# Two heads' final retention states multiplied out in the last norm, and y's last piece stored as two

## The chip, the cores and the metric

The kernel runs on one core of one Trainium2 chip. The metric is device time in microseconds (us) of one execution. The kernel before takes 1508.17 us (median of 3 runs, 1507.63 to 1508.33). One further execution was profiled; it took 1509.1 us. In the profile, PE is the matmul engine (TensorE), PEld its weight loads, DVE is VectorE, ACT ScalarE, POOL GpSimd and SP the engine that issues every DMA of this kernel. Nearly every instruction carries the line L318, the line of a recording helper, so instructions are told apart by tile names and shapes.

## The reference

One layer of a hybrid decoder over 16 meta tokens, 256 prompt tokens and 8 x 4 sample tokens. A norm and one input projection feed two groups of heads, RWKV-7 time mixing (16 heads, handled in 8 pairs) and retention (4 heads of width 256). Their outputs go through one output projection and a residual add, then a norm, a SwiGLU feed-forward with residual, and a last norm whose result is y. The states of all heads are outputs too. The part that matters here is the final retention state of the prompt:

```python
def retention_chunk(q, k, v, S, log_gamma):
    ...
    o_inter = jnp.einsum('bihd,bhde->bihe', q, S) * inter_scale[None, :, :, None]
    k_scale = jnp.exp(log_gamma[:, None] * (C - 1.0 - idx)[None, :])
    S_new = jnp.exp(log_gamma * C)[None, :, None, None] * S + jnp.einsum('bjhd,hj,bjhe->bhde', k, k_scale, v)
    return o_intra + o_inter, S_new

y_prompt = rms_norm(h_p, norm_final)[:, N_META:]
```

Since the prompt starts from a zero state, the last state of a head is one sum over all 272 prompt positions of decayed k times v: a 256 x 256 matrix per head. No other value of the step is computed from it.

## The kernel before, in words

Activations stand feature-major: 128 features on the partitions, tokens along the free axis (304 with the meta tokens, 288 without). All large products are made of 128 x 128 weight tiles. The weights come as one stream `big` in pieces of 128 x 512 (`wr`), five buffers deep; ACT rounds a piece to a short float (`wh`), DVE takes the rest (`wl`), and three matmuls per tile (`wh` with high and low part of x, `wl` with the high part) add up in a PSUM tile `acc`. `mm` are the other PSUM tiles (six banks), and nearly all other SBUF tiles lie in one arena (`arena_dt.float`, and `arena_dt.float32r` for rounded ones).

The order of work is written by a planner in a dry run (`Plan`). One main program walks through the weight stream: input projection, output projection in two halves (over the first 8 and the last 8 feature tiles of the mixed outputs), then for each of 11 groups the gate, up and down products. All other work, for example `pair(p)` for two RWKV heads and `ret(h)` for one retention head, is a stream, a generator with a rank. Whenever PE would take its next step, the planner lets the ready stream of lowest rank go on, and the main program only when none is ready. `RRANK` holds the ranks of the four retention heads; pair p has rank 1 + p. What results is one fixed order per engine. Arena places are chosen afterwards from the lifetimes.

`ret(h)` runs as follows. It transposes k and v on PE; ACT writes them to SBUF as `kt` (k scaled by the decay) and `vt`. PE makes the scores (six matmuls, 256, 144 and 48 columns wide, twice each); DVE multiplies q by the decay (`qh`), and ACT spreads it into `qz`. Then six matmuls of 128 x 256 in full fp32 give kt times vt in one `mm` bank, the final prompt state: ACT copies it to `so` and SP stores it in `rtp` (256 KB a head). `s0r` are the 8 samples' given states (four loads of 512 KB a head): sixteen matmuls of 32 x 256 multiply `qz` with them, the first four of each eight with the first half of `qz`. After that come the head's own outputs (two tiles `o`), a norm and the gate. The heads 2 and 3 run at the end of the input projection, together with the last pairs; the first product of the output projection begins when pair 7 is done, and its eight tiles of x are rounded (`xh`, `xl`) just ahead of it.

The end: the feature tile 15 of the last down product is added to the residual in three parts, each is squared on ACT, and `rstd_from` sums the squares over the features with matmuls one column wide, six in number, takes a square root (ACT) and a reciprocal (DVE), and spreads the result over all partitions with three matmuls of 96 columns. `bridge(n)` issues n products of ones with ones of 128 columns, whose result nothing reads: four of them stand ahead of the six, one behind them. Then `final` multiplies y's 16 feature tiles by the result on DVE, in 9 pieces (two of one tile, seven of two), and SP stores each piece when it is done.

Of the kernel before, what the change touches and what calls it, by code (L numbers as in the profile page):

```python
# [15 lines left out]
P = 128  # L16
D = 2048
KT = D // P
# [13 lines left out]
RD = 256  # L32
# [9 lines left out]
ACC = 2  # L42
LATE = 20000
WARM = 10
BRIDGE = 4
WR = 5
WCOLS = 512
WS = 5
# [1 line left out]
PMAX = 4  # L50
AHEAD = 4
RETS = 2
HELD = 2
RAHEAD = 2
RSTART = (-1, -1, 6, 5)
RRANK = (20, 21, 22, 2.5)
ORDER = "p0 p1 p2 r0 g0 p3 p4 r1 p5 p6 p7 g1 r2 g2 g3 r3"


# [548 lines left out]
class Step:  # L608


    def __init__(self, tc, I, O, ctx, rooms, draft, log):
        self.tc, self.nc, self.I, self.O = tc, tc.nc, I, O
        self.rooms, self.draft = rooms, draft
        pool = lambda n, b, **k: ctx.enter_context(tc.tile_pool(name=n, bufs=b, **k))
        self.lp = pool("lows", 1)
        self.cp = pool("const", 1)
        self.wp = pool("weights", 1)
        self.mp = pool("scratch", 1)
        self.ap_ = pool("acc", ACC, space=bass.MemoryType.PSUM)
        self.pp = pool("psum", 1, space=bass.MemoryType.PSUM)  # L620
        self.n, self.tags = 0, {}
        self.plan = pl = Plan(self.nc, rooms, draft, log, (lambda i: i) if draft else tc.keep_in_program_order)
        self.sp = pl.sp
        if not draft:
            self.arena = {dt: self.mp.tile([P, -(-(r.size - 16) // 64) * 64 + 16 if dt == F32 else r.size], dt, tag=f"arena_{dt}", name=f"arena_{dt}")
                          for dt, r in rooms.items()}
        self.pe, self.dve, self.act, self.pool = pl.pe, pl.dve, pl.act, pl.pool
        pl.outside = {v.name for v in (*I.values(), *O.values())}
        self.outs, self.later, self.held = [], [], []
        self.live = 0  # L630
        self.done = set()
        self.filled = set()
# [910 lines left out]
    def new_state(self, h, b2, s0, skh, svh):  # L1543
# [16 lines left out]
            dve.scalar_tensor_tensor(sd, sd, self.gam4[h], pt, op0=ALU.mult, op1=ALU.add)  # L1560
        self.put(self.O["rts"][h, b2], s0)

    def held_states(self, h, ks, vt):

        skh, svh = yield from self.exact(ks, vt)
        for b2 in range(NB // 2):
            s0 = self.t([P, 2, 2, RD], "s0n")
            self.sp.dma_start(s0, self.I["s0r"][h, b2])
            yield
            yield from self.new_state(h, b2, s0, skh, svh)  # L1570

    def ret(self, h, q, k, v):
        cst, act, dve, pe = self.cv, self.act, self.dve, self.pe
# [15 lines left out]
        kt = self.t([P, 3, RD], "kt")  # L1589
        vt = self.t([P, 3, RD], "vt")  # L1590
        ks = self.t([P, RD], "ks")
        sam = slice(P - 32, P)
        for src in k, v:
            for tiles in (0, 1), (2,):
                pt = self.ps(2 * len(tiles) + 1 if src is v else 3 * len(tiles) + (2 in tiles))
                for j, i in enumerate(tiles):
                    for d in range(2):
                        c = j * RD + d * P
                        pe.transpose(pt[:, c:c + P], src[:, d, KEYS[i][0]:KEYS[i][0] + P], ident)
                yield  # L1600
                if src is v:
                    n = len(tiles)
# [13 lines left out]
        pt = self.ps(7)  # L1616
# [8 lines left out]
        for d in range(2):  # L1625
            act.copy(qz[:, d, :, :4], four(qh[:, d]))

        pt = self.ps(7)
        for d in range(2):
            for i in range(3):  # L1630
                pe.matmul(pt[:, d * RD:(d + 1) * RD], kt[:, i, d * P:(d + 1) * P], vt[:, i, :],
                          start=i == 0, stop=i == 2)
        yield
        so = self.t([P, 2, RD], "so")
        act.copy(so, pt.rearrange("p (d e) -> p d e", d=2))
        self.put(self.O["rtp"][h], so)

        now = h < HELD
        if now:
# [2 lines left out]
        for g in range(2):  # L1642

            pt = self.ps(9)
            for d in range(2):
                for j in range(4):
                    b = 4 * g + j
                    pe.matmul(pt[32 * j:32 * j + 32, :RD], qz[:, d].rearrange("p b c -> p (b c)")[:, 32 * b:32 * b + 32], s0s[b // 2][:, d, b % 2, :],
                              start=d == 0, stop=d == 1, tile_position=(0, 32 * j))
# [16 lines left out]
        for e in range(2):  # L1666
            es = slice(e * P, (e + 1) * P)
            pt = self.ps(5)
# [63 lines left out]
            yield  # L1732
            self.dve.tensor_add(ssq, ssq, sq)

    def rstd_from(self, ssq, uses, more=None):


        ps = self.ps(4 if more is None else 7)
        n = TO // 3
        for c in range(3):  # L1740
            self.pe.matmul(ps[:n, c:c + 1], ssq[:, c * n:(c + 1) * n], self.ones[:, :1], start=True, stop=more is None)
            if more is not None:
                self.pe.matmul(ps[:n, c:c + 1], more[:, c * n:(c + 1) * n], self.ones[:, :1], start=False, stop=True)
        if more is None:
            yield
            rs = yield from self.rsqrt(ps[:n, :3], 1.0 / D, RMS_EPS)
        else:
            self.bridge(1)
            yield
            rs = self.t([n, 3], "rsz")  # L1750
            self.act.activation(rs, ps[:n, :3], AF.Sqrt, scale=1.0 / D, bias=self.eps[RMS_EPS][:n])
            yield
            self.dve.reciprocal(rs, rs)
            yield
        ps = self.ps(3 + uses)
        for c in range(3):
            self.pe.matmul(ps[:, c * n:(c + 1) * n], rs[:, c:c + 1].to_broadcast([n, P]), self.cv("id", n, 0, n),
                           start=True, stop=True)
        yield
        return ps[:, :TO]  # L1760

    def bridge(self, n=BRIDGE):

        pt = self.ps(n)
        for _ in range(n):
            self.pe.matmul(pt[:, :P], self.ones, self.ones, start=True, stop=True)

    def fill(self, k):

# [63 lines left out]
    def ffn_jobs(self):  # L1833
# [25 lines left out]
        def down_post(m, fin):  # L1859
            def g(acc):  # L1860
                hm = self.ht[m // 4][:, m % 4, :]
                if fin and m == KT - 1:

                    sq = self.t([P, TO], "sq2")
                    third = [slice(c * TO // 3, (c + 1) * TO // 3) for c in range(3)]
                    for c in third:
                        dve.tensor_add(hm[:, c], hm[:, c], acc[:, c])
                    for c in third:
                        act.activation(sq[:, c], hm[:, c], AF.Square)
                    self.bridge()  # L1870
                    yield
                    yield from self.final(sq)
                    return
                dve.tensor_add(hm, hm, acc[:, :TO])
                if fin:
                    if m == 0:
                        self.ssq3 = self.t([P, TO], "ssq3")

                        root = self.t([P, 1], "root")
                        act.activation(root, self.ones[:, :1], AF.Sqrt)  # L1880
                    yield
                    yield from self.sumsq(self.ssq3, hm, m == 0)
                    yield
                    act.activation(hm, hm, AF.Copy, scale=self.pv("gfin", m))
            return g
# [11 lines left out]
                                need=lambda f=f1 - 1 - (f1 == FT): ("act", f) in self.done))  # L1897
        return jobs

    def final(self, sq):  # L1900
        rstd = yield from self.rstd_from(self.ssq3, 9, sq)
        hm = self.ht[-1][:, 3, :]
        self.act.activation(hm, hm, AF.Copy, scale=self.pv("gfin", KT - 1))
        for m, n in [(0, 1), (1, 1)] + [(m, 2) for m in range(2, KT, 2)]:
            h = self.ht[m // 4][:, m % 4:m % 4 + n, :]
            self.dve.tensor_mul(h, h, rstd[:, None, :].to_broadcast([P, n, TO]))
            self.sp.dma_start(self.O["y"][:, m:m + n, :], h)

    def build(self, gam4):
        self.gam4 = gam4  # L1910
# [78 lines left out]
```

## Time and profile before

| what | value |
|---|---|
| three timed runs | 1508.17, 1507.63, 1508.33 us |
| profiled execution | 1509.1 us, of which the span from first to last instruction 1507.3 us |
| granted TensorE clock, mean | 0.997 |
| PE busy | 1493.5 us, 99% of the span, 11438 matmul records |
| DVE, ACT, POOL busy | 1086.2, 884.7, 31.9 us |
| chain of work that ended last | PE 95%, DVE 3%, ACT 1% |
| DMA | 258.57 MB, mean 172 GB/s |

A full fp32 matmul leaves two records in the profile, so a row with x12 is six matmuls. Rows of the timeline merge neighbouring instructions of one kind and name the first one's shape: a row "128x256" may hold matmuls of 144, 48 or 32 columns that follow it. A row's start is exact; the end of a matmul is modelled, so what a group of matmuls takes is read from its start to the start of the next row. In the text, pitch means this.

### The profile page before, as it was taken

The page shows a single profiled execution, that of the slowest core. Times are in us where ns is not written, and L with a number is a line of the kernel's source. Part 1 is how long each engine was busy: PE and PEld are TensorE (multiplying, and loading weights), DVE is VectorE, ACT ScalarE, POOL GpSimd, SP SyncE. Part 2 cuts the span into 40 slices and gives each one's busy share as a digit, 9 for nine tenths or more (in the row PEclk, how much of TensorE's full clock was granted, in tenths as well). Part 3 has the DMA queues.
Part 4 walks back from the last instruction along what each step waited for, and adds up shares of the span by engine and source line. Part 5 has one row for each costly group of instructions (what it writes and reads, how often), then busy time and mean ns, then how long its engine had stood idle before and what let it go on. Part 6 is the DMA issues. An engine that isn't in the chain of part 4 may idle for free.

```text
span 1507.3 us, 31980 instructions
## 1 busy us (share of the span) xinstructions
PE 1493.5 (99%) x11438; PEld 1475.3 (98%) x11438; DVE 1086.2 (72%) x2768; ACT 884.7 (59%) x2109; POOL 31.9 (2%) x165
## 2 busy tenths in 40 slices
PE   9999999999999999999999999999999999999997
PEld 8999999999999989999999999999999999999997
DVE  6989997999999668876656555656565656565657
ACT  6786778787875875567544444444444444444445
POOL 0010000000000000000000000000000000000000
PEclk9999999999999999999999999999999999999998
DMA  7545444545444368866655555555555555555563
GB/s 233 180 144 162 148 155 118 163 156 152 141 123 141 103 226 288 282 179 203 194 173 170 168 175 171 169 177 164 174 168 171 172 170 170 177 165 177 165 176 119
DMA packets 138784, 258.57 MB, mean 172 GB/s; under 512 B 16257, under 2 KB 22657, under 8 KB 138625
## 3 DMA queue, kind: packets, MB, share of 16 engines
q1 hardware_dynamic: 138624, 256.52, 55.8%
q8 instruction: 91, 1.49, 0.4%
q14 instruction: 69, 0.56, 0.1%
HBM read 242.18 MB, written 14.28 MB: 170 GB/s over the span
## 4 chain that ended last, share of the span: by engine, by line
PE 95%; DVE 3%; ACT 1%; issue 0%; DMA 0%; SPq 0%; DVEq 0%; ACTq 0%
PE acc L318 84%; PE mm L318 11%; DVE arena_dt.float L318 2%; ACT arena_dt.float L318 1%; DVE wl L318 1%; DMA arena_dt.float<-xT 0%; SPq L318 0%; ACT wh L318 0%; ACT arena_dt.float32r L318 0%; DVE arena_dt.float32r L318 0%; DVE xl L318 0%; DVEq L1985 0%; ACT xh L318 0%; ACT shout L318 0%; DVEq L318 0%
## 5 line engine op out<-in xcount | busy, mean ns | idle before, releaser
L318 PE MATMUL acc<-xh,wh 128*128 128x288 f32 (+2 forms) x2592 | 781.1, 301 | 1.5 <-ACT wh L318 1.5
L318 PE MATMUL acc<-xh,wl 128*128 128x288 f32 (+2 forms) x2592 | 763.9, 295 | 0.5 <-DVE wl L318 0.5
L318 PE MATMUL acc<-xl,wh 128*128 128x288 f32 (+2 forms) x2592 | 760.5, 293 | 0.0
L318 ACT CAST wh<-wr 128x512 fp32r<-128x512 f32 (+1 forms) x827 | 504.0, 617 | 347.9 <-PE acc L318 305.0
L318 DVE TENSOR_TENSOR wl<-wr,wh 128x512 fp32r<-128x512 f32 (+1 forms) x827 | 559.9, 686 | 125.7 <-ACT wh L318 121.0
L318 PEld LDWEIGHTS acc<-xh,wh 128*128 128x128 f32 x2592 | 486.7, 188 | 5.7 <-issue 2.7
L318 PEld LDWEIGHTS acc<-xl,wh 128*128 128x128 f32 x2592 | 486.3, 188 | 3.0 <-issue 1.9
L318 PEld LDWEIGHTS acc<-xh,wl 128*128 128x128 f32 x2592 | 485.5, 187 | 1.6 <-DVE wl L318 1.3
L318 PE MATMUL acc<-arena_dt.float32r,wh 128*128 128x288 f32 x1408 | 273.7, 292 | 0.2 <-DVE arena_dt.float L318 0.2
L318 PEld LDWEIGHTS acc<-arena_dt.float32r,wh 128*128 128x128 f32 x1408 | 223.9, 188 | 0.6 <-DVE arena_dt.float L318 0.4
L318 PE MATMUL acc<-arena_dt.float32r,wl 128*128 128x288 f32 x704 | 205.8, 292 | 0.0
L318 DVE TENSOR_TENSOR arena_dt.float<-acc,arena_dt.float 128x288 f32<-128x288 f32 (+4 forms) x181 | 72.7, 420 | 148.0 <-PE acc L318 147.4
L318 DVE TENSOR_TENSOR arena_dt.float<-arena_dt.float 128x288 f32<-128x288 f32 (+21 forms) x658 | 159.6, 279 | 10.2 <-ACT arena_dt.float L318 7.9
L318 PE MATMUL mm<-arena_dt.float 128*128 128x128 f32 (+7 forms) x1120 | 162.0, 299 | 0.8 <-ACT arena_dt.float32r L318 0.6
L318 ACT ACTIVATE arena_dt.float<-arena_dt.float 128x288 f32<-128x288 f32 (+7 forms) x229 | 97.3, 432 | 103.8 <-DVE arena_dt.float L318 102.4
L318 DVE TENSOR_TENSOR arena_dt.float<-arena_dt.float,acc 128x288 f32<-128x288 f32 (+1 forms) x210 | 94.6, 451 | 85.2 <-PE acc L318 82.8
L318 PEld LDWEIGHTS mm<-arena_dt.float 128*128 128x128 f32 (+1 forms) x1120 | 138.2, 181 | 7.5 <-issue 1.7
L318 PEld LDWEIGHTS acc<-arena_dt.float32r,wl 128*128 128x128 f32 x704 | 132.1, 188 | 0.0
L318 ACT COPY arena_dt.float<-mm 64x64 f32<-64x64 f32 (+11 forms) x338 | 95.1, 290 | 43.8 <-PE mm L318 39.7
L318 ACT COPY arena_dt.float<-arena_dt.float 128x8 f32<-128x8 f32 (+8 forms) x267 | 62.4, 283 | 26.7 <-DVE arena_dt.float L318 25.4
L318 ACT CAST arena_dt.float32r<-arena_dt.float 128x288 fp32r<-128x288 f32 (+6 forms) x117 | 49.7, 429 | 40.3 <-DVE arena_dt.float L318 39.9
L318 DVE TENSOR_TENSOR arena_dt.float32r<-arena_dt.float,arena_dt.float32r 128x288 fp32r<-128x288 f32 (+6 forms) x116 | 52.3, 452 | 17.9 <-ACT arena_dt.float32r L318 16.0
(68 smaller groups left out, 575.1 us busy)
## 6 DMA issues: line engine op xcount, KB each, us to landing
wr<-big SPq DMA_DIRECT2D x823, 256.0 KB, 2.8
arena_dt.float<-s0r SPq DMA_DIRECT2D x24, 512.0 KB, 5.9
out_rts<-arena_dt.float SPq DMA_DIRECT2D x16, 512.0 KB, 4.3
arena_dt.float<-s0w SPq DMA_DIRECT2D x16, 256.0 KB, 3.2
arena_dt.float<-xT SPq DMA_DIRECT2D x4, 576.0 KB, 7.1
arena_dt.float<-lora SPq DMA_DIRECT2D x16, 128.0 KB, 2.7
out_rws<-arena_dt.float SPq DMA_DIRECT2D x8, 256.0 KB, 3.4
out_y<-arena_dt.float SPq DMA_DIRECT2D x7, 288.0 KB, 2.4
```

The source lines that it names most:

```text
L318: return self._plan.keep(f(*a, **k))
```

## The change

The multiplication kt times vt moves into a function of its own (`key_values`). The heads 0 and 1 call it where it stood. The heads 2 and 3 only note kt and vt, and `last_states` does the rest in the last norm: for the head noted first, three of the six matmuls stand where the four products of ones stood, the other three where the single one stood; for the other head all six come behind the three spreading matmuls. `bridge` is gone. The two `so` copies are ACT's, the two stores are issued between y's pieces, behind tile 1 and behind tile 11. The last piece of y, two tiles, is cut into two of one tile each. The rank of head 3 becomes 23.

```diff
-BRIDGE = 4
+LASTS = 2
-RRANK = (20, 21, 22, 2.5)
+RRANK = (20, 21, 22, 23)
...
+    def key_values(self, pt, kt, vt, parts):
+
+        for c in parts:
+            d, i = divmod(c, 3)
+            self.pe.matmul(pt[:, d * RD:(d + 1) * RD], kt[:, i, d * P:(d + 1) * P], vt[:, i, :], start=i == 0, stop=i == 2)
...
-        pt = self.ps(7)
-        for d in range(2):
-            for i in range(3):
-                pe.matmul(pt[:, d * RD:(d + 1) * RD], kt[:, i, d * P:(d + 1) * P], vt[:, i, :],
-                          start=i == 0, stop=i == 2)
-        yield
-        so = self.t([P, 2, RD], "so")
-        act.copy(so, pt.rearrange("p (d e) -> p d e", d=2))
-        self.put(self.O["rtp"][h], so)
+        if h < LASTS:
+            pt = self.ps(7)
+            self.key_values(pt, kt, vt, range(6))
+            yield
+            so = self.t([P, 2, RD], "so")
+            act.copy(so, pt.rearrange("p (d e) -> p d e", d=2))
+            self.put(self.O["rtp"][h], so)
+        else:
+            self.ends.append((h, kt, vt))
...
-    def rstd_from(self, ssq, uses, more=None):
+    def rstd_from(self, ssq, uses, more=None, states=None):
...
         else:
-            self.bridge(1)
+            next(states)
             yield
             rs = self.t([n, 3], "rsz")
...
-    def bridge(self, n=BRIDGE):
-
-        pt = self.ps(n)
-        for _ in range(n):
-            self.pe.matmul(pt[:, :P], self.ones, self.ones, start=True, stop=True)
+    def last_states(self, i):
+
+        h, kt, vt = self.ends[i]
+        pt = self.ps(7)
+        for c in range(0, 6, 3):
+            self.key_values(pt, kt, vt, range(c, c + 3))
+            yield
+        so = self.t([P, 2, RD], "so")
+        self.act.copy(so, pt.rearrange("p (d e) -> p d e", d=2))
+        yield
+        self.sp.dma_start(self.O["rtp"][h], so)
+        yield
...
-                    self.bridge()
+                    states = self.last_states(0)
+                    next(states)
                     yield
-                    yield from self.final(sq)
+                    yield from self.final(sq, states)
...
-    def final(self, sq):
-        rstd = yield from self.rstd_from(self.ssq3, 9, sq)
+    def final(self, sq, states):
+        rstd = yield from self.rstd_from(self.ssq3, 10, sq, states)
+        more = self.last_states(1)
+        next(more)
+        next(more)
+        next(states)
         hm = self.ht[-1][:, 3, :]
         self.act.activation(hm, hm, AF.Copy, scale=self.pv("gfin", KT - 1))
-        for m, n in [(0, 1), (1, 1)] + [(m, 2) for m in range(2, KT, 2)]:
+        next(more)
+        for m, n in [(0, 1), (1, 1)] + [(m, 2) for m in range(2, KT - 2, 2)] + [(KT - 2, 1), (KT - 1, 1)]:
             h = self.ht[m // 4][:, m % 4:m % 4 + n, :]
             self.dve.tensor_mul(h, h, rstd[:, None, :].to_broadcast([P, n, TO]))
             self.sp.dma_start(self.O["y"][:, m:m + n, :], h)
+            if m == 1:
+                next(states)
+            if m == 10:
+                next(more)
```

PE's order is the same in both kernels up to the four 288-column products of a pair (mm_1942). Here the first of the two heads had its state product. Before (mm_1939 are the scores, mm_1943 the state, mm_1949 transposes of the other head, mm_1952 the first products of qz with the given states):

```order
L318 MATMUL mm_1939_7938<-arena_dt.float_73 128x256 x2
L318 MATMUL mm_1939_7938<-arena_dt.float_73 128x144 x2
L318 MATMUL mm_1939_7938<-arena_dt.float_73 128x48 x2
L318 MATMUL mm_1942_7948<-arena_dt.float32r 128x288 x4
L318 MATMUL mm_1943_7956<-arena_dt.float_73 128x256 x6
L318 MATMUL mm_1949_7968<-cst_323,arena_dt.float_73 128x128 x4
L318 MATMUL mm_1952_7974<-arena_dt.float_73 32x256 x8
```

And now (mm_1944 and mm_1947 are the two sets of qz products):

```order
L318 MATMUL mm_1939_7938<-arena_dt.float_73 128x256 x2
L318 MATMUL mm_1939_7938<-arena_dt.float_73 128x144 x2
L318 MATMUL mm_1939_7938<-arena_dt.float_73 128x48 x2
L318 MATMUL mm_1942_7948<-arena_dt.float32r 128x288 x4
L318 MATMUL mm_1944_7956<-arena_dt.float_73 32x256 x8
L318 MATMUL mm_1947_7971<-arena_dt.float_73 32x256 x8
L318 MATMUL mm_1949_7981<-arena_dt.float32r,sums_326 128x288 x2
```

The state is gone, and the products with qz, which ACT writes, follow at once. The second head's stretch of PE was, from its scores (mm_1974) on:

```order
L318 MATMUL mm_1974_8040<-arena_dt.float_73 128x256 x2
L318 MATMUL mm_1974_8040<-arena_dt.float_73 128x144 x2
L318 MATMUL mm_1974_8040<-arena_dt.float_73 128x48 x2
L318 MATMUL mm_1977_8056<-arena_dt.float_73 128x256 x6
L318 MATMUL mm_1978_8063<-arena_dt.float32r,sums_326 128x288 x2
L318 MATMUL mm_1981_8072<-arena_dt.float_73 32x256 x8
```

It is now, with the scores in mm_1972:

```order
L318 MATMUL mm_1972_8035<-arena_dt.float_73 128x256 x2
L318 MATMUL mm_1972_8035<-arena_dt.float_73 128x144 x2
L318 MATMUL mm_1972_8035<-arena_dt.float_73 128x48 x2
L318 MATMUL mm_1976_8049<-arena_dt.float_73 32x256 x8
L318 MATMUL mm_1979_8065<-arena_dt.float_73 32x256 x8
L318 MATMUL mm_1980_8075<-arena_dt.float32r 128x288 x4
```

The state and the summing product that stood between scores and qz products are no longer there. ACT's order ahead of that head's two qz copies (128x8x4) is now:

```order
L318 COPY arena_dt.float_73<-mm_1960_8006 128x288
L318 ACTIVATE arena_dt.float_73<-arena_dt.float_73 128x576
L318 COPY arena_dt.float_73<-mm_1962_8016 128x512
L318 ACTIVATE arena_dt.float_73<-arena_dt.float_73 128x288
L318 COPY arena_dt.float_73<-mm_1967_8025 128x256
L318 CAST arena_dt.float32r<-arena_dt.float_73 128x288
L318 COPY arena_dt.float_73<-arena_dt.float_73 128x8x4 x2
```

A square of two tiles, a copy and a square stand behind the copy of the other head's output, and a copy and a rounding follow ahead of the qz copies. At the end, PE had these rows behind the last product of the weight stream, in mm_4321 and mm_4323 the products of ones:

```order
L318 MATMUL acc_19937<-arena_dt.float32r,wl_19884 128x288
L318 MATMUL mm_4321_19961<-ones_78 128x128 x4
L318 MATMUL mm_4322_19966<-ones_78,arena_dt.float_73 96x1 x6
L318 MATMUL mm_4323_19973<-ones_78 128x128
L318 MATMUL mm_4325_19977<-cst_323,arena_dt.float_73 128x96 x3
```

And has now, with one head's state in mm_4317 and the other's in mm_4321:

```order
L318 MATMUL acc_19919<-arena_dt.float32r,wl_19866 128x288
L318 MATMUL mm_4317_19943<-arena_dt.float_73 128x256 x3
L318 MATMUL mm_4318_19947<-ones_78,arena_dt.float_73 96x1 x6
L318 MATMUL mm_4317_19943<-arena_dt.float_73 128x256 x3
L318 MATMUL mm_4320_19959<-cst_323,arena_dt.float_73 128x96 x3
L318 MATMUL mm_4321_19963<-arena_dt.float_73 128x256 x6
```

The five products of ones are replaced by six state products, and six more stand last. SP's stores at the end were two of out_y with 128x288 and seven with 128x576; they are now:

```order
L318 DMA out_y<-arena_dt.float_73 128x288 x2
L318 DMA out_rtp<-arena_dt.float_73 128x512
L318 DMA out_y<-arena_dt.float_73 128x576 x5
L318 DMA out_rtp<-arena_dt.float_73 128x512
L318 DMA out_y<-arena_dt.float_73 128x576
L318 DMA out_y<-arena_dt.float_73 128x288 x2
```

Two stores of 256 KB stand among y's, and y's last 576-column piece is two of 288.

More of the change, by code (lines that the diff above doesn't have):

```diff
@@ L628, in __init__ @@
         pl.outside = {v.name for v in (*I.values(), *O.values())}
-        self.outs, self.later, self.held = [], [], []
+        self.outs, self.later, self.held, self.ends = [], [], [], []
         self.live = 0
```

## Prediction

> **What bounds the kernel now.** I read the page first, then busy time in stretches of the program, then the timeline at the two places where instructions leave and arrive. The first two lines are the page's (busy time; shares of the chain that ended last), then three rows of the stretches (bounds, length, busy time and instructions by engine, clock, DMA share, GB/s).
>
> ```profile
> PE 1493.5 (99%) x11438; PEld 1475.3 (98%) x11438; DVE 1086.2 (72%) x2768; ACT 884.7 (59%) x2109; POOL 31.9 (2%) x165
> ...
> PE 95%; DVE 3%; ACT 1%; issue 0%; DMA 0%; SPq 0%; DVEq 0%; ACTq 0%
> ...
> 540.00:550.00 10.00, 10.00 (x87) 8.03 (x86) 5.11 (x14) 7.41 (x21) 0.58 (x1) 1.00 1.05 396
> 550.00:560.00 10.00, 10.00 (x80) 8.49 (x82) 5.59 (x14) 7.31 (x20) 0.00 (x0) 1.00 0.34 124
> 750.00:1000.00 250.00, 250.00 (x1942) 250.00 (x1941) 149.66 (x270) 108.36 (x187) 0.00 (x0) 1.00 0.59 171
> ```
>
> PE is the bound from start to end, at full clock, and it is dense even between 540 and 560 us, where only small products of the last pairs and the heads 2 and 3 run. So a matmul taken out there is worth its whole pitch, as long as the next instruction is ready. Later, 1942 records in 250 us give 0.129 us for one weight product. Only the last 12.6 us, behind the weight stream, have another bound.
>
> **What is removed in the middle.** The timeline of PE (start, length, engine, operation, records):
>
> ```profile
> 541.83 1.90 PE L318 MATMUL mm<-arena_dt.float 128*128 128x256 f32 x12
> 543.55 0.77 PE L318 MATMUL mm<-arena_dt.float32r 128*128 128x288 f32 x4
> 544.16 2.75 PE L318 MATMUL mm<-arena_dt.float 128*128 128x256 f32 x12
> 546.75 0.60 PE L318 MATMUL mm<-cst,arena_dt.float 128*128 128x128 f32 x4
> 547.28 1.07 PE L318 MATMUL mm<-arena_dt.float 128*32 128x256 f32 x16
> 548.28 0.54 PE L318 MATMUL mm<-arena_dt.float32r,sums 128*128 128x288 f32 x2
> 548.75 1.07 PE L318 MATMUL mm<-arena_dt.float 128*32 128x256 f32 x16
> ...
> 553.15 4.56 PE L318 MATMUL mm<-arena_dt.float 128*128 128x256 f32 x24
> 557.35 0.61 PE L318 MATMUL mm<-arena_dt.float32r,sums 128*128 128x288 f32 x2
> ```
>
> The first head's scores run from 541.83 to 543.55 (1.72), its state from 544.16 to 546.75: 2.59 us. The row at 553.15 is the second head's scores and state together, 4.20; less 1.72 for the scores, its state is 2.48. Out go **5.07 us**. Two rounded products of 288 columns take 0.47 (548.28 to 548.75) where twice 0.129 would be 0.26, so an island of them among fp32 work costs some 0.2. The new order has two islands fewer between 544 and 563 (one joins its neighbour, and the three weight products that stood alone ahead of the last head output join theirs): **0.4 us**, between 0 and 0.6.
>
> The two ACT copies and two 256 KB stores that leave this stretch free nothing that PE waited for: I cost them at nothing.
>
> **What loses its cover.** Between scores and qz products stood the state; now PE comes to the qz products early. ACT's timeline:
>
> ```profile
> 544.53 0.35 ACT L318 COPY arena_dt.float<-arena_dt.float 128x32 f32<-128x32 f32 x2
> ...
> 553.22 0.68 ACT L318 ACTIVATE arena_dt.float<-arena_dt.float 128x576 f32<-128x576 f32 x1
> 553.80 0.48 ACT L318 ACTIVATE arena_dt.float<-mm,omu 128x288 f32<-128x288 f32 x1
> 554.19 0.36 ACT L318 COPY arena_dt.float<-mm 128x256 f32<-128x256 f32 x1
> 554.44 0.44 ACT L318 CAST arena_dt.float32r<-arena_dt.float 128x288 fp32r<-128x288 f32 x1
> 554.77 0.45 ACT L318 ACTIVATE arena_dt.float<-arena_dt.float 128x288 f32<-128x288 f32 x1
> 555.12 0.33 ACT L318 COPY arena_dt.float<-arena_dt.float 128x32 f32<-128x32 f32 x2
> ```
>
> The first head's two qz copies begin at 544.53; the first of them is over near 544.75, and PE would be there at 544.16. ACT's order up to there is unchanged, so PE waits **0.6 us** (0.4 to 0.9). Behind the waiting product stand PE's whole queue, pair 7 first.
>
> At the second head the old copies began at 555.12, 2.0 after the scores, which take 1.72. In the new order ACT has ahead of these copies the 576-wide square, a copy of 512, a square, a copy of 256 and a rounding; by the pitches of the rows above (0.58 for the wide square, 0.42 for 0.5 us pieces, 0.25 to 0.4 for the others) some 2.3 us, and the square itself waits for the copies of the other head's output. PE has behind that output only the summing product, six transposes and the scores. I take **1.0 us** of waiting, between 0.3 and 1.6.
>
> Then pair 7, whose result opens the output projection:
>
> ```profile
> 552.58 0.51 PE L318 MATMUL mm<-arena_dt.float32r,sums 128*128 128x288 f32 x2
> 561.77 0.38 PE L318 MATMUL acc<-xh,wh 128*128 128x288 f32 x1
> 562.25 0.99 PE L318 MATMUL mm<-arena_dt.float 128*128 128x256 f32 x6
> 563.28 0.38 PE L318 MATMUL acc<-xh,wh 128*128 128x288 f32 x1
> 562.38 0.82 DVE L318 TENSOR_TENSOR xl<-arena_dt.float,xh 128x288 fp32r<-128x288 f32 x2
> ```
>
> Its chain from the summing product (552.58) to the rounded x (562.38 plus 0.82) takes 10.6 us. PE needs the tiles of this x at the 18th product of the projection. Before, PE's first product came 9.2 after 552.58. Now 2.48 are gone, four transposes (0.53) and the second head output (1.03, 562.25 to 563.28) come in, an island less (0.2), the wait of 1.0: 9.0, and 18 times 0.129 makes 11.3. The margin is 0.7: no wait, at most 1.0 if ACT is later than I think.
>
> The middle gives 5.07 + 0.4 - 0.6 - 1.0 = **3.9 us**; bounds 2.0 (both waits long, pair 7 late) and 5.0 (short waits 0.7, islands 0.6), or 5.7 with no wait at all.
>
> **What is added at the end.** The end on PE, ACT and DVE:
>
> ```profile
> 1494.74 1.05 PE L318 MATMUL mm<-ones 128*128 128x128 f32 x8
> 1495.63 1.10 PE L318 MATMUL mm<-ones,arena_dt.float 128*96 128x1 f32 x12
> 1496.59 0.47 PE L318 MATMUL mm<-ones 128*128 128x128 f32 x2
> 1497.38 0.88 PE L318 MATMUL mm<-cst,arena_dt.float 96*128 96x96 f32 x6 [0.32 <-DVE arena_dt.float L318]
> 1495.23 0.63 ACT L318 ACTIVATE arena_dt.float<-arena_dt.float 128x96 f32<-128x96 f32 x3 [0.38 <-DVE arena_dt.float L318]
> 1496.77 0.26 ACT L318 ACTIVATE arena_dt.float<-mm,omu 96x3 f32<-96x3 f32 x1 [0.91 <-PE mm L318]
> 1497.06 0.17 DVE L318 RECIPROCAL arena_dt.float<-arena_dt.float 96x3 f32<-96x3 f32 x1 [1.54 <-ACT arena_dt.float L318]
> 1498.30 5.47 DVE L318 TENSOR_TENSOR arena_dt.float<-arena_dt.float,mm 128x288 f32<-128x288 f32 x9 [1.06 <-PE mm L318]
> ```
>
> Four products of ones took 0.89 (1494.74 to 1495.63), and the one-column sums followed without a wait. Three state products are half of 2.59, 1.30: the sums begin 0.41 later, at 1496.04, and end 0.96 later at 1497.00. The other three then run to 1498.30, while root and reciprocal are over by 1497.23 + 0.41 = 1497.64. So the spreading products begin at 1498.30 instead of 1497.38: **+0.9 us** (0.5 if a ready operand saves some of their 0.9; 1.1 if switching costs). The six products of the other head stand behind them, off the path: done near 1501.8, copied by 1502.4, and SP comes to that store only behind y's tile 11, near 1503.4.
>
> The stores (three stretches of the end, same columns as above, then the times from issue to landing of y's nine stores):
>
> ```profile
> 1499.50:1501.00 1.50, 0.00 (x0) 0.00 (x0) 1.50 (x3) 0.00 (x0) 0.00 (x0) 0.50 0.81 284
> 1501.00:1506.00 5.00, 0.00 (x0) 0.00 (x0) 2.77 (x5) 0.00 (x0) 0.00 (x0) 0.50 1.01 385
> 1506.00:1507.30 1.30, 0.00 (x0) 0.00 (x0) 0.00 (x0) 0.00 (x0) 0.00 (x0) 0.50 0.02 5
> ...
> DMA to landing us min/median/max: 1.8/2.3/2.7
> ```
>
> From 1501 to 1506 the DMA engines are full at 385 GB/s, although DVE ends at 1503.77: the last stretch is bound by bytes, not by DVE. Two stores of 262144 bytes are 0.524 MB, at 385 GB/s **+1.36 us**. A part could fall into the idle 0.19 of the first 1.5 us, 0.3 at most; the two small pieces at the end may lose about as much as they did at the start, where 0.81 of the engines moved 284 GB/s (350 at full use). I set both against each other. Cutting the last piece in two gains nothing while a queue stands ahead of it: between -0.3 and +0.2. The Trainium skill, DMA: Bandwidth & Descriptors, section "Anatomy of one DMA — SWDGE (gpsimd) path", counts about 2 us fixed for each DMA of that path and 436 GB/s for the bytes, which speaks against cutting; by its rate the two stores would be an estimated 1.2 us and the whole change 0.16 better. The rows show 1.8 to 2.7 us from issue to landing, overlapped, and no 436, so I stay with 385.
>
> The end costs 0.9 + 1.36 = **2.3 us**, between 1.5 and 2.9. Together: -3.9 + 2.3 = **-1.6 us**. The profiled execution, 1509.1 us with 1507.3 of span and 1.8 around it, would be 1507.5 with a span of 1505.7. It lies 0.93 above the median of the runs shown, so the forecast for that is 1508.17 - 1.6, **1506.6 us**.
>
> **Rivals.** (1) The cover is not needed. If ACT comes to the qz copies as early as PE does, the middle gives 5.07 + 0.4 = 5.5 and the end 2.3, sum -3.2: 1505.0; with 0.3 of the new bytes in idle DMA time, -3.5: 1504.7. For it: ACT was 73% busy there (7.41 and 7.31 of 10) and loses two copies. Against: the first wait follows from an ACT row that does not move. (2) Slower: the weights come late. Between 570 and 620 us the samples' states are loaded a second time and stored, together with the weight stream:
>
> ```profile
> 599.41 0.62 ACT L318 CAST wh<-wr 128x512 fp32r<-128x512 f32 x1 [2.97 <-DMA wr<-big]
> ...
> DMA packets 7271, 15.68 MB, mean 314 GB/s; under 512 B 733, under 2 KB 1757, under 8 KB 7266
> ```
>
> ACT already waits 2.97 us for a weight piece. PE stays dense since ACT is four roundings ahead of it, 48 products or 6.2 us. One load of 512 KB takes 1.36 us at 385 GB/s, and SP's new order has fewer weight pieces among the eight loads than the old one (19 instead of 25). If four more loads stand ahead of one piece than before, the wait becomes 2.97 + 5.4 = 8.4 and PE stands still for 2.2; while the queue stays full, 0.7 more at each of four further pieces, 5.0 in all: -1.6 + 5.0, 1511.6. It decides once ACT's wait there passes 6.2. Against it: 0.5 MB of stores leaves this queue, and PE shows no wait in this stretch so far. (3) The change does nothing: kt and vt of two heads must stay for 950 us, and if the arena had to give them room by waiting elsewhere, the 3.9 would shrink to about the 2.3 of the end: 1508.2.
>
> **How the numbers follow.** The forecast has 0.70, (1) 0.20, (2) 0.06, (3) 0.04. A measurement of this kernel can tell about 0.2% (3.0 us) from no change. The forecast and (3) lie within it, but for 0.01 of (3) that may end slower; (1) lies beyond on the fast side, (2) on the slow one: faster 0.20, same 0.73, slower 0.07. The forecast's own range is 1505.3 to 1508.0. For 8 in 10 it reaches to the better end of (1), below, and to the worst sum of my bounds, -2.0 + 2.9, above: **1504.5 to 1509.0**.
>
> **What would show it.** In the new profile: no row of 128x256 behind the four 288-column products near 544; PE idle time ahead of both sets of qz products, released by ACT, 0.6 and 1.0; the first weight product of 288 columns behind the heads about 4 us sooner; the last product of the stream 3.9 earlier; from it to the first multiplication of y 0.9 more; the DMA engines full until the end and the last store landing 1.4 later against DVE's start. Wrong it is if PE shows no wait there, if a wait at the first products of the output projection appears, or if the end costs under 1.5.

## The result: 24 us slower, and none of it where the change works

The changed kernel takes 1532.67 us (median of 5 runs, 1531.87 to 1533.73) against 1508.33 (5 runs, 1507.63 to 1509.36): a ratio of 1.016, 95% interval 1.0145 to 1.0175. The forecast was 1506.6 with no measurable change, so it missed by 26 us.

The profile page after, with the lines that answer to those shown of before (busy time; shares of the chain that ended last), then three stretches with the same bounds as before and a fourth (bounds, length, busy time and instructions of PE, PEld, DVE, ACT and POOL, clock, DMA share, GB/s):

```profile
PE 1516.4 (99%) x11428; PEld 1498.7 (98%) x11428; DVE 1087.0 (71%) x2769; ACT 883.7 (58%) x2109; POOL 32.1 (2%) x165
...
PE 92%; DVE 3%; ACT 2%; DMA 1%; issue 1%; SPq 0%; DVEq 0%; POOL 0%; ACTq 0%
...
540.00:550.00 10.00, 9.58 (x93) 8.22 (x91) 6.13 (x17) 8.14 (x24) 0.58 (x1) 1.00 1.05 398
550.00:560.00 10.00, 9.27 (x87) 8.01 (x87) 6.83 (x18) 7.68 (x20) 0.41 (x2) 1.00 0.19 68
750.00:1000.00 250.00, 250.00 (x1878) 250.00 (x1877) 145.34 (x262) 104.84 (x181) 0.00 (x0) 1.00 0.54 166
1000.00:1470.00 470.00, 470.00 (x3528) 470.00 (x3527) 272.48 (x490) 199.10 (x344) 0.00 (x0) 1.00 0.54 165
```

Between 750 and 1000 us nothing was edited. PE is busy all the time in both kernels, at full clock in both, and yet it gets through 1878 weight products where it got through 1942. That is 250 / 1878 = 0.1331 us from one to the next in place of 0.1287, and it goes on nearly to the end of the stream. Busy share and clock do not show it; the count does.

The long stretch of weight products begins behind the last product of the samples' states. Its first product, its last one and the end of the span, before and after:

```profile
724.08 1.02 PE L318 MATMUL mm<-arena_dt.float 128*128 128x512 f32 x2
724.53 0.70 PE L318 MATMUL acc<-xh,wh 128*128 128x288 f32 x1
...
1494.61 0.29 PE L318 MATMUL acc<-arena_dt.float32r,wl 128*128 128x288 f32 x1
```

```profile
721.39 1.02 PE L318 MATMUL mm<-arena_dt.float 128*128 128x512 f32 x2
721.85 0.70 PE L318 MATMUL acc<-xh,wh 128*128 128x288 f32 x1
...
1516.81 0.29 PE L318 MATMUL acc<-arena_dt.float32r,wl 128*128 128x288 f32 x1
```

The stretch has 5,961 products in both. After the change it begins 2.68 us sooner (724.53 less 721.85) and lasts 794.96 us in place of 770.08, which is 24.88 more. From its last product to the end of the span it is 15.19 us (1532.0 less 1516.81) in place of 12.69, 2.50 more. -2.68 + 24.88 + 2.50 is the whole difference of the spans, 24.7 (the spans are printed to 0.1 us, and the last term is good to that). Without the middle number the change is worth -0.2 us.

**Two rhythms, and the trace of before has both.** Starts of successive weight products, in ns, from the traces, each list from the middle of a stretch (the products come in threes: hi by hi, lo by hi, hi by lo):

```
before, near 800 us:  129 128 129 130 128 129 129 129 129 129 128 129   mean 128.89
after,  near 800 us:  131 133 136 131 133 136 131 133 136 131 133 136   mean 133.33
```

The second is an exact round of three products in 400.0 ns. I call them the short and the long rhythm. In before's timeline around 690 us, one 128-column transpose turns the first into the second:

```profile
688.83 0.29 PE L318 MATMUL acc<-xh,wh 128*128 128x288 f32 x1
688.96 0.29 PE L318 MATMUL acc<-xl,wh 128*128 128x288 f32 x1
689.09 0.29 PE L318 MATMUL acc<-xh,wl 128*128 128x288 f32 x1
689.22 0.29 PE L318 MATMUL acc<-xh,wh 128*128 128x288 f32 x1
...
689.61 0.27 PE L318 MATMUL mm<-cst,arena_dt.float 128*128 128x128 f32 x1
...
690.52 0.30 PE L318 MATMUL acc<-xh,wh 128*128 128x288 f32 x1
690.65 0.29 PE L318 MATMUL acc<-xl,wh 128*128 128x288 f32 x1
690.78 0.30 PE L318 MATMUL acc<-xh,wl 128*128 128x288 f32 x1
690.92 0.30 PE L318 MATMUL acc<-xh,wh 128*128 128x288 f32 x1
```

Three products take 0.39 ahead of it (688.83 to 689.22) and 0.40 behind it (690.52 to 690.92). From 666 to 724 us, where products of other shapes (islands, for short) stand between the weight products, both kernels change from one rhythm to the other many times. Then come the 5,961 products with no island among them, and whichever rhythm the last island left goes on to within 25 us of their end: before drew the short one, after the long one.

### The profile page after: what moved, and what is told of

It reads as the page before. It is cut to its first block, busy times and chain, and to the rows that moved or that the text cites. A ratio compares the mean times of both kernels' runs of the same rounds, so it can differ in the third digit from the quotient of the medians.

```text
span 1532.0 us, 31962 instructions
## 1 busy us (share of the span) xinstructions
PE 1516.4 (99%) x11428; PEld 1498.7 (98%) x11428; DVE 1087.0 (71%) x2769; ACT 883.7 (58%) x2109; POOL 32.1 (2%) x165
## 4 chain that ended last, share of the span: by engine, by line
PE 92%; DVE 3%; ACT 2%; DMA 1%; issue 1%; SPq 0%; DVEq 0%; POOL 0%; ACTq 0%
PE acc L318 82%; PE mm L318 10%; DVE arena_dt.float L318 1%; ACT arena_dt.float L318 1%; DMA wr<-big 1%; DVE wl L318 1%; ACT wh L318 0%; ACT xh L318 0%; DMA arena_dt.float<-xT 0%; DVE xl L318 0%; SPq L318 0%; DVE arena_dt.float32r L318 0%; ACT arena_dt.float32r L318 0%; DVEq L2008 0%; POOL arena_dt.float L318 0%
## 5 line engine op out<-in xcount | busy, mean ns | idle before, releaser
L318 PE MATMUL acc<-arena_dt.float32r,wh 128*128 128x288 f32 x1408 | 281.5, 295 | 0.2 <-DVE arena_dt.float L318 0.2
```

The costliest lines, as they stand in the source:

```text
L318: return self._plan.keep(f(*a, **k))
```

## The experiments

Theory A: either rhythm keeps itself up until an island or a wait of PE breaks it, what breaks it decides which one follows, and the change did no more than alter what stood ahead of the long stretch. Theory B: something that the change adds (transfers, tiles that stay longer, products) slows every weight product. Theory C: what counts is the number of matmul records on PE ahead of a stretch, so that the rhythm alternates with it. Each ratio below is to runs of the kernel before taken beside that kernel.

**The split of y's last piece alone,** on the kernel before:

```diff
-        rstd = yield from self.rstd_from(self.ssq3, 9, sq)
+        rstd = yield from self.rstd_from(self.ssq3, 10, sq)
...
-        for m, n in [(0, 1), (1, 1)] + [(m, 2) for m in range(2, KT, 2)]:
+        for m, n in [(0, 1), (1, 1)] + [(m, 2) for m in range(2, KT - 2, 2)] + [(KT - 2, 1), (KT - 1, 1)]:
```

> The kernel before with y's last piece as two (14 and 15 apart) and nothing else: TensorE's order is untouched. Theory A (a 288-column product has two rhythms, 129.0 and 133.3 ns from one to the next, each of which keeps itself up until a product of another form or a wait comes between; the 5,961 products behind the last such product draw one of them, and the change only altered the draw): the long stretch stays at 129.0, the time within 1.5 us of 1508.3. Theory B (what the change adds, its transfers or its places in memory, slows every weight product by 4.3 ns): only if the split is the cause, 1532; else 1508. This run also prices the split itself: the forecast had the end full of transfers, so within 1 us of no change.

1509.65 us against 1508.84, ratio 1.0002 (0.9993 to 1.0012). The split neither causes the loss nor gains anything, as the forecast had it.

**The moved states alone:** the change with `RRANK` left at `(20, 21, 22, 2.5)` and y's pieces as before.

> The kernel before with the last two heads' state products moved to the last norm, but the last head's rank left at 2.5 and y's pieces as before. Theory A: the stretch is at one rhythm or the other as a whole, 129.0 or 133.3, and the time is near 1507 or near 1531, nothing between; the islands in front of it show both rhythms, as in both kernels. Theory B (the moved products and their tiles slow the weight products): 133.3 and 1531.

Ten executions of this one program took 1508.06 to 1510.20 us eight times and 1534.33 and 1534.60 twice, with nothing between and the same clock (0.997 to 0.999). The ratio of the eight is 1.0002 (0.9992 to 1.0013). The profiled one, of 1508.24, has the short rhythm, 128.89 ns over the stretch. So the moved work does not slow the products, and one program can come out at either time: against theory B. The two long executions were not profiled; that they had the long rhythm is taken from their times alone.

**The last head's rank alone,** on the kernel before, no state moved:

```diff
-RRANK = (20, 21, 22, 2.5)
+RRANK = (20, 21, 22, 23)
```

> The kernel before with the last head's rank at 23 and nothing else. Theory A: the order of the small products ahead of the long stretch is another one, so its rhythm is drawn anew: 1507 to 1509 with 129.0 or 1531 to 1534 with 133.3, nothing between; it may come out either way from run to run. Theory B (the moved products slow the stretch): 1508.

1534.86 us, ratio 1.0168 (1.0155 to 1.0182); the stretch runs at 133.33. Here nothing was moved to the end. By shape, PE's products stand in another order between 547 and 620 us only and in the same order behind that, and the loss is the same. Theory B fails here too. The three edits of the change, one by one, give nothing, mostly nothing, and the whole loss.

**An island put into the changed kernel.** A product of no use is put ahead of the gate product of tile 4, nine weight products behind the last state product. First a rounded one, 512 columns as two times 256:

```diff
+            if k == 0 and key == ("gate", 4):
+                self.island(hi[:, o:o + P])
...
+        self.pe.matmul(pt.rearrange("p (a b) -> p a b", a=2), w, self.xflat, start=True, stop=True)
```

> The changed kernel with one rounded 512-column product (no use is made of it) ahead of the gate product of tile 4, some 200 products into the long stretch; cost 0.2 to 0.5 us. Theory A: the rhythm is drawn anew there: 133.3 before it, and behind it either 129.0 to the end (1508 to 1509) or 133.3 again (1533); the rounded products of the output projection all left 129.0, so 129.0 is the likelier. Theory B: 133.3 before and behind it, 1533.

1534.21 us, ratio 1.0165 (1.0149 to 1.018): the long rhythm ahead of it and behind it. The short rhythm behind it, called the likelier, did not come (and the place is nine products into the stretch, not some 200). That alone would suit theory B. Which island leaves what had to be counted.

**Two counts of islands,** 124 in each run, on the kernel before:

```diff
+            if k == 0 and (key[0] in ("gate", "up") and key[1] > 3 or key[0] == "down" and key[2] % 4 == 0):
+                self.island(hi[:, o:o + P])
```

> The kernel before with a product of no use ahead of each gate and up tile from tile 4 on and ahead of every fourth down tile, 124 in all, four kinds in turn: rounded 512 columns, unrounded 512, unrounded 128, a 128-column transpose. Theory A: the 48 products behind each are at 129.0 or at 133.3, changing from one to the next, both rhythms many times in one run with the same tiles in the same places; the counts by kind say what a kind leaves. Theory B: all at 129.0, since nothing of the change is in it. Theory C (it is the number of rows on TensorE ahead of a stretch): a fixed alternation with the rows added. Time: 124 times 0.2 to 0.5 us over 1508, and up to 26 us more.

> The kernel before with an unrounded product of constants ahead of each gate and up tile from tile 4 on and of every fourth down tile, 124 in all, of 256, 192, 384 and 64 columns in turn. Theory A: a given width leaves nearly always the same rhythm, as 512 (129.0) and 128 (133.3) columns did; which one is not foreseen: it goes by a few nanoseconds in the start of the products behind it. If one of 256 columns or fewer leaves 129.0, it would set the rhythm for less than 0.86 us. Theory B: all at 129.0.

The times, 1569.36 and 1570.17 us, are those of the added products and of the long rhythms. The rhythm that the products behind each island settle into, by the rhythm ahead of it (the first island of either run, which met a rhythm still settling, is left out):

```
island                        short stays  short to long  long stays  long to short
rounded, 2 x 256 columns           8             0            22            0
unrounded, 512 columns            10             0             0           21
unrounded, 384                    31             0             0            0
unrounded, 256                     0             0             0           30
unrounded, 192                    31             0             0            0
unrounded, 128                     0            31             0            0
unrounded, 64                      0            31             0            0
transpose, 128                     0             0            23            8
```

Nothing of the change is in these kernels, and the same tiles in the same places run at one rhythm or the other, by the island ahead: against theory B. Theory C wants an alternation with the number of records; islands of 192, 384 and 64 columns add two each and met the short rhythm, and the first two kept it each time where the third ended it each time. The kinds come in a fixed turn, so 384, 192, 128 and 64 columns met the short rhythm only and 256 the long one only. The rounded island hands on what it meets, which fits the run before. In the narrow count, a 64-column island (start and length as in the other timelines):

```profile
747.31 0.42 PE L318 MATMUL acc<-arena_dt.float32r,wh 128*128 128x288 f32 x2
747.57 0.29 PE L318 MATMUL acc<-arena_dt.float32r,wl 128*128 128x288 f32 x1
747.70 0.42 PE L318 MATMUL acc<-arena_dt.float32r,wh 128*128 128x288 f32 x2
747.96 0.29 PE L318 MATMUL acc<-arena_dt.float32r,wl 128*128 128x288 f32 x1
748.09 0.33 PE L318 MATMUL mm<-cst,ones 128*128 128x64 f32 x2
...
748.57 0.30 PE L318 MATMUL acc<-arena_dt.float32r,wl 128*128 128x288 f32 x1
748.71 0.43 PE L318 MATMUL acc<-arena_dt.float32r,wh 128*128 128x288 f32 x2
748.97 0.30 PE L318 MATMUL acc<-arena_dt.float32r,wl 128*128 128x288 f32 x1
```

Three products take 0.39 ahead (747.31 to 747.70, 747.57 to 747.96) and 0.40 behind (748.57 to 748.97).

**The island that leaves the short rhythm,** in the changed kernel at the same place (the line in `island`):

```diff
+        self.pe.matmul(pt, self.ones, self.cst[:, :512], start=True, stop=True)
```

> The changed kernel with one unrounded 512-column product of constants (no use is made of it) ahead of the gate product of tile 4, some ten weight products behind the last state product, at a cost of 0.86 us (428 + 28 + 535 ns from start to start in place of one product's 133). In the probe this product left the 129.0 rhythm 31 times of 31, 21 of them out of the 133.3 one. Theory A: 5,950 products at 129.0 in place of 133.3 take 25.5 us off 1532.7 and the product adds 0.9: 1507.5 to 1509. Theory B (what the change adds slows the products): 133.3 goes on, 1533.5.

1508.31 us (11 runs, 1506.78 to 1510.31), ratio 0.9992 (0.9983 to 1.0001). One useless product, which costs 0.86 us (428 + 28 + 535 ns from start to start in place of 133), takes 24 us off. The same stretch as above, of this kernel:

```profile
750.00:1000.00 250.00, 250.00 (x1941) 250.00 (x1941) 149.26 (x270) 109.19 (x188) 0.00 (x0) 1.00 0.57 171
```

**The island that leaves the long rhythm,** in the kernel before, twice: ahead of gate tile 4 and, in a later run, 48 products further on, ahead of up tile 4:

```diff
+        self.pe.matmul(pt[:, :P], self.ones, self.ones, start=True, stop=True)
```

> The kernel before, nothing of the change in it, with one unrounded 128-column product of ones in the same place; in the probe it left the 133.3 rhythm 31 times of 31. Cost by itself 0.2 us (109 + 30 + 217 ns in place of one product's 129). Theory A: the whole stretch at 133.3, 5,950 times 4.3 ns: 1508.4 + 25.6 + 0.2 = 1533 to 1535. Theory B: 1508.6.

1510.56 us, ratio 1.0007 (0.9998 to 1.0016): a miss. The starts around it were 133 135 129 130 130 129, island, 133 130 134 131 134 128: the rhythm was still settling from the state product nine products earlier, while each island of that kind in the count had met a settled short rhythm. That this is why the short one came back is argued from the starts; the second run tests what the same product does behind a settled rhythm:

> The kernel before with the unrounded 128-column product of ones ahead of the up product of tile 4, 48 products later than in the run that missed. There it met a rhythm that was still settling (133 135 129 130 130 ns ahead of it); in the probe it met a settled 129.0 each time. Theory A: here it meets a settled 129.0 as in the probe and leaves 133.3: 5,904 products times 4.3 ns, 1508.4 + 25.4 + 0.2 = 1533 to 1535. If the 129.0 goes on, what stands ahead of a product does not set the rhythm and theory A falls.

1534.27 us (4 runs, 1534.14 to 1534.45), ratio 1.0164 (1.015 to 1.0178). Its stretch:

```profile
750.00:1000.00 250.00, 250.00 (x1877) 250.00 (x1876) 146.22 (x264) 104.77 (x180) 0.00 (x0) 1.00 0.55 166
```

So the kernel before, with one product of 0.2 us added, loses what the changed kernel loses, and the changed kernel, with one of 0.86 us, loses nothing. Theory A is shown in both directions.

**The changed kernel with the rhythm set, and its end mended.** The island is the 256-column one, and two of the first state's last three products go behind the products that spread the norm's factor:

```diff
-                    states = self.last_states(0)
+                    states = self.last_states(0, (0, 3, 4, 6))
...
                            start=True, stop=True)
+        if more is not None:
+            next(states)
         yield
```

> The changed kernel with an unrounded 256-column product of constants ahead of the gate product of tile 4 (in the probe it left 129.0 31 times of 31; cost 0.43 us) and, in the last norm, two of the three products of the first state's second half put behind the products that spread the norm's factor: these started 0.5 us late behind them (1520.58, with the reciprocal done at 1519.90). Theory A: 129.0 to the end, 0.43 under the run with 512 columns, and y's first multiplication 0.4 to 0.5 us sooner: 1507.0 to 1508.0, 0.05 to 0.1 per cent under the kernel before.

1507.24 us (11 runs, 1506.21 to 1509.96) against 1509.31, ratio 0.999 (0.9981 to 0.9999): under both kernels, by an amount at the edge of what can be told from none. PE at the end of its profile:

```profile
1490.23 1.46 PE L318 MATMUL mm<-arena_dt.float 128*128 128x256 f32 x6
1491.52 1.10 PE L318 MATMUL mm<-ones,arena_dt.float 128*96 128x1 f32 x12
1492.48 0.68 PE L318 MATMUL mm<-arena_dt.float 128*128 128x256 f32 x2
1493.34 0.88 PE L318 MATMUL mm<-cst,arena_dt.float 96*128 96x96 f32 x6 [0.18 <-DVE arena_dt.float L318]
```

The spreading products now start when the reciprocal is there, 3.11 us behind the first product after the stream (1493.34 less 1490.23), where it was 3.64 (1520.58 less 1516.94, rows below).

**Where the streamed rows begin.** The narrow count again, with the 288 columns beginning at element 16 of their place in memory:

```diff
-SHIFT_X = [20] * KT
+SHIFT_X = [16] * KT
-SHIFT_A = [20] * 11
+SHIFT_A = [16] * 11
```

> The kernel of the narrow probe (products of 256, 192, 384 and 64 columns in turn ahead of 124 tiles), with the rows that the weight products stream beginning at element 16 of their place in memory in place of 20, both for the norm's output and for the gated products. Nothing of TensorE's order changes. If the two rhythms belong to the order of the instructions alone, the stretches stay at 129.0 (256, 192, 384) and 133.3 (64). If the place of the streamed rows has a part in them, the rhythms themselves have other lengths, or a width leaves another one; the weight products of the input projection, whose 288 columns begin at element 16 too, took some 131 ns in the profile of before.

1574.34 us in its one run. All four widths leave one and the same rhythm: 131.1 ns in each of the 123 stretches that no wait interrupts, with 128 to 134 ns from one start to the next. The two rhythms are not a matter of the instructions' order alone. From element 20 the products have a rhythm better by 2.2 ns and one worse by 2.2; from element 16 this run shows one only.

## Why the prediction was wrong, point by point

**The step that failed** stands in its first part: "Later, 1942 records in 250 us give 0.129 us for one weight product." That was read as a property of a weight product, and the sum then let 770 us of untouched stream cost the same as before, without a term or a rival for it. The term measured +24.88 us, and the last product of the stream, which the prediction wanted 3.9 earlier, came 22.2 later (1516.81 less 1494.61). By the settled rhythms the term is up to 5,961 times 4.44 ns, 26.5 us; most of the rest is missing since PE stops for a moment some 170 products ahead of the end, and behind that the rhythm is the other one in both kernels, long before and short after. In the changed one it is this:

```profile
1493.05 0.43 PE L318 MATMUL acc<-arena_dt.float32r,wh 128*128 128x288 f32 x2
...
1493.45 0.43 PE L318 MATMUL acc<-arena_dt.float32r,wh 128*128 128x288 f32 x2
...
1493.85 0.64 PE L318 MATMUL acc<-arena_dt.float32r,wh 128*128 128x288 f32 x2
...
1495.16 0.53 PE L318 MATMUL acc<-arena_dt.float32r,wh 128*128 128x288 f32 x2 [0.16 <-DVE arena_dt.float L318]
...
1496.44 0.42 PE L318 MATMUL acc<-arena_dt.float32r,wh 128*128 128x288 f32 x2
...
1496.83 0.42 PE L318 MATMUL acc<-arena_dt.float32r,wh 128*128 128x288 f32 x2
```

Three products take 0.40 ahead of this place (1493.05 to 1493.45) and 0.39 behind it (1496.44 to 1496.83). The place holds a group that comes late by itself (1493.85) and a wait of 0.16 us; which of the two changes the rhythm is not shown. In y_split, move_only and after_island_512 the same place left the short rhythm as it was. None of the three rivals held this; a fourth, "the rhythm of the long stretch is drawn anew, +25 us, one chance in three" (5 of the last 15 stretches ahead of it have the long one), could have been priced from before's rows up to 724 us.

**The middle,** forecast -3.9, measured -4.2 at the first out-projection products and -2.7 at the long stretch. PE's timeline after:

```profile
542.11 1.90 PE L318 MATMUL mm<-arena_dt.float 128*128 128x256 f32 x12
543.83 0.77 PE L318 MATMUL mm<-arena_dt.float32r 128*128 128x288 f32 x4
545.02 1.93 PE L318 MATMUL mm<-arena_dt.float 128*32 128x256 f32 x32 [0.42 <-ACT arena_dt.float L318]
...
551.05 1.90 PE L318 MATMUL mm<-arena_dt.float 128*128 128x256 f32 x12
553.68 1.93 PE L318 MATMUL mm<-arena_dt.float 128*32 128x256 f32 x32 [0.73 <-ACT arena_dt.float L318]
...
597.16 0.70 PE L318 MATMUL mm<-arena_dt.float32r 128*128 128x512 f32 x2 [0.57 <-DVE arena_dt.float32r L318]
602.79 0.72 PE L318 MATMUL mm<-arena_dt.float32r 128*128 128x512 f32 x2 [0.26 <-ACT arena_dt.float32r L318]
```

- No state product (a 128*128 row of 128x256) stands behind the four 288-column products any more: right.
- Both sets of qz products wait for ACT: right, 0.42 and 0.73 where 0.6 and 1.0 were said.
- Pair 7 brings no wait at the projection's first products: right. The product behind the third one, 563.28 before, starts at 559.08: 4.2 sooner, where about 4 was said.
- That gain then shrinks by 1.5 up to the long stretch. Of it, 0.83 is the waits at 597 and 602, for rounded operands of the samples' states. Rival 2 looked at this stretch, but for late weight pieces under the weight products; late were the operands of the islands between them. A third wait, 0.16 at 668.90, is for `wl`, so of rival 2's kind but small. The other 0.5 I have not broken down.

**The end,** forecast +2.3, measured +2.50. PE and DVE after, then two stretches:

```profile
1516.94 1.46 PE L318 MATMUL mm<-arena_dt.float 128*128 128x256 f32 x6
1518.23 1.10 PE L318 MATMUL mm<-ones,arena_dt.float 128*96 128x1 f32 x12
1519.20 1.54 PE L318 MATMUL mm<-arena_dt.float 128*128 128x256 f32 x6
1520.58 0.81 PE L318 MATMUL mm<-cst,arena_dt.float 96*128 96x96 f32 x6
...
1519.73 0.17 DVE L318 RECIPROCAL arena_dt.float<-arena_dt.float 96x3 f32<-96x3 f32 x1 [2.01 <-ACT arena_dt.float L318]
1521.42 5.54 DVE L318 TENSOR_TENSOR arena_dt.float<-arena_dt.float,mm 128x288 f32<-128x288 f32 x10 [1.51 <-PE mm L318]
...
1524.00:1530.00 6.00, 0.00 (x0) 0.00 (x0) 2.96 (x6) 0.58 (x1) 0.00 (x0) 0.84 1.00 384
1530.00:1532.00 2.00, 0.00 (x0) 0.00 (x0) 0.00 (x0) 0.00 (x0) 0.00 (x0) 0.50 0.28 93
```

From the first product behind the stream to y's first multiplication it is 4.48 us (1521.42 less 1516.94), before 3.56: 0.92, where 0.9 was said. From there to the end of the span 10.58 in place of 9.00: 1.58, where 1.36 was said, with the DMA engines full at 384 GB/s.

**What is left of the forecast.** With the short rhythm in both kernels, the change is what it was called, no measurable difference: the changed kernel with the 512-column island stands at 0.9992, its 0.86 us included. But the likeliest case had 0.70, and no case of the forecast contained what happened.

## What to carry to other kernels

A pitch that is read off one long stretch is a measurement of that stretch and not a constant: look through the trace for the same instruction at another pitch, and where there is one, give the long stretch both prices, whatever the edit is. Compare counts of instructions in equal windows and not busy shares; a stream that is 100% busy at full clock can still be 3% slower. And a kernel whose time hangs on such a draw should set it on purpose, with a product of known effect ahead of the stretch, before two versions of it are compared.

## What the runs showed of the hardware

- A stream of rounded 128x128 by 128x288 products, each with its own weight load, has two lasting rhythms here, 128.89 and 133.33 ns, at the same granted clock of 1.00. Each lasts for thousands of products, through changes of weight buffers, accumulators and input tiles.
- A single product of another width can change the one into the other; so did a moment's stop of PE late in the stream, with a wait of 0.15 or 0.16 us in it, in two runs, and in three others the same stop did not. At the boundary of a tile and behind a settled rhythm, an unrounded product of 192 to 512 columns left the short one 123 times of 123, one of 64 or 128 columns the long one 62 times of 62. The kernel's own 512-column state products left either. From the first weight product behind the island to the second it is 530 or 535 ns behind the added 512-column island and 534 to 540 behind the state products. 535 stood ahead of the short rhythm 21 times in the count and ahead of the long one in the kernels before and after, so this start does not decide by itself; what does stays open.
- Where the streamed rows begin decides which rhythms there are: two were seen from element 20, one of 131.1 ns from element 16.
- What in TensorE makes the two rhythms stays open. The Trainium skill, TensorE: Matmul & The Clock Gate, section "Back-to-back issue gap", has the spacing in such a stream set by the product and the weight load together, and gives N / 2.4 + 2.5 ns for a product by itself, for 288 columns an estimated 122.5. Both rhythms lie above that estimate, by 6.4 and 10.8 ns; that one width can have two lasting spacings is not stated there, and the runs show it.
